# Gate and up products of four feed-forward layers as Strassen's seven block products, with the down product cut into five parts

## The chip, the cores and the metric

One core of one Trainium2 chip runs the whole program as a single launch. The metric is the device time of that launch in microseconds (us); smaller is better. The engines that matter here are PE (TensorE, the matrix engine, with PEld for its weight loads), DVE (VectorE), ACT (ScalarE), POOL (GpSimd) and SP (SyncE, which issues most DMAs).

## The reference, cut to what matters

A model of two blocks on 512 tokens of width 1024, all in fp32. The first block has two layers, each of them: a feed-forward, a mixer of three branches (Fourier, dilated attention, differential attention), and a second feed-forward. So there are four feed-forwards in the first block, and the change rewrites these. The second block (a mixer with delta rule and window attention, a cross attention to a memory, one more feed-forward) follows.

```python
D_MODEL = 1024; SEQ = 512; D_FF = 2816
def swiglu(h, w_gate, w_up, w_down):
    return (jax.nn.silu(h @ w_gate) * (h @ w_up)) @ w_down
# first block, per layer l
x = x + 0.5 * swiglu(rmsnorm(x, g_ffn1[l]), w_ffn1_gate[l], w_ffn1_up[l], w_ffn1_down[l])
...   # mixer
x = x + 0.5 * swiglu(rmsnorm(x, g_ffn2[l]), w_ffn2_gate[l], w_ffn2_up[l], w_ffn2_down[l])
```

## The kernel before

The activations lie transposed: `x[c]` is 128 channels by 512 tokens, c from 0 to 7. Every fp32 operand of a product is split into a high and a low fp32r part (`split`, line 299: ACT copies the high part, DVE subtracts it from the source for the low part), and each 128x128 block of weights takes three matmuls of 512 columns: high by high, high by low, low by high (`mm3`, line 351). Weights are fetched from HBM by SP into `raw` tiles of 128x1024 (pool of 3), and split into `whi` and `wlo` tiles of 128x512 (pools of 5 each). Most other tiles come from one pool of 128x512 tiles, `pg`, with NB = 63 of them (line 45).

A feed-forward (`ffn_task`, line 708) works in two halves of 11 column tiles of 128 out of the 22 of D_FF. For each column tile, `ffn_half` (line 675) forms the gate product and the up product, each 8 blocks of the inner dimension by 3 matmuls. Their operand is `us`, x times its gain, without the norm's factor; `evac` multiplies both results by the norm's row `rb` (`mul_rb`), takes silu on ACT, multiplies, and splits the product into `hs`. After a half comes its part of the down product: for each of 8 channel tiles, 11 blocks by 3 matmuls, added to x by DVE. In the second half `pre_chunk` (line 442) follows each channel tile: it makes the next stage's `us[c]` and adds its squares for the next norm, on POOL. The norm itself (`norm_task`, line 431) runs beside the first product of the next stage, `wide` (line 473), which makes four column tiles at a time.

The order of instructions is that of the program's own driver (`drive`, line 236): tasks are generators with a priority, they yield when their operands are due by a running estimate (`note`, line 192), and `acq`/`rel` (line 274) count the tiles of `pg` that a task may hold. The mixers start with a count of NB - 22 (line 829), the second block's mixer with NB - 30 less what the memory task holds (line 1447). Then a scheduler places the instructions on the engines, each of which runs its own in order. Two tasks, `setup_second` (line 1188: clears a scratch area in HBM by one DMA of 4.1 MB, loads masks, makes sine and cosine tables) and `memory` (line 2070: norm and transposes of the memory's 256 rows), are started with the last feed-forward of the first block and spread over it by waits of 20 to 60 us of planned time.

## Time and profile before

| | |
|---|---|
| time, median of 3 runs | 3449.64 us (3449.59 to 3451.47) |
| time of the profiled execution | 3459.29 us |
| its span | 3457.5 us |
| PE busy | 3356.0 us, 97% |
| PE weight loads busy | 2835.2 us, 82% |
| DVE busy | 1905.8 us, 55% |
| ACT busy | 1369.1 us, 40% |
| POOL busy | 337.6 us, 10% |

Busy times are of the profiled execution. Matmuls overlap each other in the pipeline, so the mean duration of one is longer than the distance from one start to the next; the distances are what a stage is made of. An instruction of DVE or ACT that waits for nothing also starts before the one ahead of it has ended. The four feed-forwards stand, by their weights' DMA issues, at about 0 to 368, 864 to 1230, 1230 to 1591 and 2088 to 2466 us.

### The profile page before, as it was taken

The page shows a single profiled execution, that of the slowest core. Times are in us where ns is not written, and L with a number is a line of the kernel's source. Part 1 is how long each engine was busy: PE and PEld are TensorE (multiplying, and loading weights), DVE is VectorE, ACT ScalarE, POOL GpSimd, SP SyncE. Part 2 cuts the span into 40 slices and gives each one's busy share as a digit, 9 for nine tenths or more (in the row PEclk, how much of TensorE's full clock was granted, in tenths as well). Part 3 has the DMA queues.
Part 4 walks back from the last instruction along what each step waited for, and adds up shares of the span by engine and source line. Part 5 has one row for each costly group of instructions (what it writes and reads, how often), then busy time and mean ns, then how long its engine had stood idle before and what let it go on. Part 6 is the DMA issues. An engine that isn't in the chain of part 4 may idle for free.

```text
span 3457.5 us, 44625 instructions
## 1 busy us (share of the span) xinstructions
PE 3356.0 (97%) x16759; PEld 2835.2 (82%) x16759; DVE 1905.8 (55%) x3644; ACT 1369.1 (40%) x2672; POOL 337.6 (10%) x325
## 2 busy tenths in 40 slices
PE   8999999999999999999999999999978889999998
PEld 7788888898888888888888987888867887788887
DVE  5444476656444444444767474545488764754344
ACT  4323445543332333234445443333354443443232
POOL 1000100000000000001000001000354433220001
PEclk9999999999999999999999999999999999999999
DMA  4533333435333333334333257333336453223232
GB/s 123 151 104 101 117 96 101 124 109 176 93 95 101 95 100 90 100 96 121 96 101 119 86 189 147 102 102 96 93 121 189 152 156 107 68 74 99 96 98 85
DMA packets 424422, 386.46 MB, mean 112 GB/s; under 512 B 31184, under 2 KB 379577, under 8 KB 424205
## 3 DMA queue, kind: packets, MB, share of 16 engines
q1 hardware_dynamic: 383584, 333.50, 32.2%
q10 hardware_dynamic: 40141, 48.54, 5.2%
q8 instruction: 131, 2.15, 0.3%
q0 software_dynamic: 480, 1.57, 0.1%
q14 instruction: 86, 0.70, 0.1%
HBM read 341.46 MB, written 37.88 MB: 110 GB/s over the span
## 4 chain that ended last, share of the span: by engine, by line
PE 90%; DVE 5%; DMA 2%; ACT 1%; issue 1%; POOL 0%; SPq 0%; ACTq 0%; DVEq 0%; POOLq 0%
PE ps L119 90%; DVE g L119 3%; DVE sm L119 1%; ACT g L119 1%; DVE wlo L119 0%; DMA raw<-in_w_ffn_gate 0%; ACT whi L119 0%; DVE tmp L119 0%; DMA g<-xinv_d 0%; DMA raw<-in_w_in 0%; DMA raw<-in_w_ffn_up 0%; DMA g<-cs_d 0%; ACT L119 0%; DMA g<-in_g_ffn 0%; DMA g<-in_x 0%
## 5 line engine op out<-in xcount | busy, mean ns | idle before, releaser
L119 PE MATMUL ps<-g,whi 128*128 128x512 f32 (+1 forms) x7776 | 2396.9, 390 | 19.7 <-ACT g L119 9.4
L119 PEld LDWEIGHTS ps<-g,whi 128*128 128x128 f32 x7776 | 1450.3, 189 | 314.1 <-ACT g L119 11.1
L119 PE MATMUL ps<-g,wlo 128*128 128x512 f32 (+1 forms) x3888 | 1508.6, 388 | 4.7 <-DVE wlo L119 2.8
L119 ACT ACTIVATE whi<-raw 128x512 fp32r<-128x512 f32 (+2 forms) x1100 | 673.0, 617 | 1347.2 <-PE ps L119 1216.8
L119 DVE TENSOR_TENSOR wlo<-raw,whi 128x512 fp32r<-128x512 f32 (+2 forms) x1038 | 706.3, 685 | 607.6 <-ACT whi L119 589.2
L119 PEld LDWEIGHTS ps<-g,wlo 128*128 128x128 f32 x3888 | 735.6, 189 | 157.2 <-DVE wlo L119 4.9
L119 DVE TENSOR_TENSOR g<-ps,g 128x512 f32<-128x512 f32 (+3 forms) x486 | 299.1, 625 | 422.9 <-PE ps L119 342.4
L119 DVE TENSOR_TENSOR g<-g,g 128x512 f32<-128x512 f32 (+3 forms) x494 | 352.9, 726 | 133.3 <-ACT g L119 124.7
L119 POOL TENSOR_TENSOR g<-g,g 128x512 f32<-128x512 f32 (+4 forms) x142 | 181.9, 1289 | 2142.7 <-ACT g L119 2088.8
L119 ACT ACTIVATE g<-g 128x512 fp32r<-128x512 f32 (+3 forms) x473 | 289.8, 617 | 206.3 <-DVE g L119 171.5
L119 PE MATMUL ps<-g,g 128*128 128x128 f32 (+6 forms) x1638 | 265.7, 310 | 19.0 <-ACT g L119 7.1
L119 PE MATMUL ps<-whi,g 128*128 128x256 f32 (+1 forms) x1184 | 259.2, 312 | 0.0
L119 PEld LDWEIGHTS ps<-g,g 128*128 128x128 f32 (+3 forms) x1638 | 224.2, 193 | 40.2 <-ACT g L119 8.5
L119 PEld LDWEIGHTS ps<-whi,g 128*128 128x128 f32 x1184 | 198.0, 193 | 11.4
L119 PE MATMUL ps<-wlo,g 128*128 128x256 f32 (+1 forms) x592 | 183.9, 311 | 0.0
L119 ACT ACTIVATE g<-ps 128x256 fp32r<-128x256 f32 (+6 forms) x231 | 95.6, 426 | 150.5 <-PE ps L119 128.2
L119 DVE SCALAR_TENSOR_TENSOR g<-ps,g 128x512 f32<-128x512 f32 x114 | 83.5, 734 | 103.7 <-PE ps L119 101.7
L119 PEld LDWEIGHTS ps<-wlo,g 128*128 128x128 f32 x592 | 114.3, 193 | 5.9
L119 POOL TENSOR_TENSOR wlo<-raw,whi 128x512 fp32r<-128x512 f32 x62 | 86.5, 1396 | 222.0 <-ACT whi L119 198.0
L119 ACT COPY g<-ps 128x512 f32<-128x512 f32 (+6 forms) x154 | 59.5, 417 | 111.2 <-PE ps L119 106.1
L119 ACT ACTIVATE g<-g,sm 128x512 f32<-128x512 f32 (+3 forms) x160 | 89.0, 579 | 31.2 <-DVE sm L119 28.3
L119 PE MATMUL ps<-ident,g 128*128 128x128 f32 (+1 forms) x491 | 79.1, 286 | 21.4 <-DVE g L119 12.2
(173 smaller groups left out, 1352.4 us busy)
## 6 DMA issues: line engine op xcount, KB each, us to landing
raw<-in_w_ffn_gate SPq DMA_DIRECT2D x87, 512.0 KB
raw<-in_w_ffn_up SPq DMA_DIRECT2D x87, 512.0 KB
raw<-in_w_in SPq DMA_DIRECT2D x80, 512.0 KB
raw<-in_w_ffn_down SPq DMA_DIRECT2D x64, 512.0 KB
raw<-in_w_gate SPq DMA_DIRECT2D x48, 512.0 KB
raw<-in_w_gate_up SPq DMA_DIRECT2D x44, 512.0 KB
raw<-in_w_ffn_down SPq DMA_DIRECT2D x64, 192.0 KB
gd<-g ACTq DMA_DIRECT2D x48, 256.0 KB
```

Of the source, the lines that this page charges most:

```text
L119: r = f(*a, **k)
```

## The change

In each of the four feed-forwards the column tiles 0 to 5 of D_FF are formed as before (tiles 0 and 1 by `wide`, tiles 2 and 3 from `us`; tiles 4 and 5 from the normed and split x that `fast_x` makes, so without the two multiplications by `rb`). The other 16 tiles are done in 8 groups of two, called quads here. For a quad the weights form a 2 by 2 block matrix (gate and up, by even and odd blocks of the inner dimension) and the tokens another (even and odd blocks, by first and second 256 tokens). Its eight block products become Strassen's seven, each of 2 x 4 x 3 = 24 matmuls of 256 columns. `fast_ops` makes the four sums of activations once per feed-forward. `fast_split` splits the weights of one product and forms four sums of weights per quad, each over 128x1024, on DVE. `fast_mm` lets several products add up in the same PSUM bank; ACT copies intermediate sums out of it, DVE adds and multiplies, `fast_end` splits the results into `hs`.

The down product is cut into five passes, over 6, 4, 4, 4 and 4 column tiles. The first four stand between the quads; only the last stands at the end. The sequence is a hand-written list of items, whose weights are split three items ahead of their matmuls. Between the second quad and the third there is no down product.

Around it: `raw` has 5 tiles for 3, `pg` 59 for 63, and a new tag `big` (4 tiles of 128x1024) serves the normed x and half of the quads' weights, and in the mixers what had tags of its own (`v`, `oa`, `vdh`, `vdl`). `setup_second` and `memory` wait until the last pass of the last of the four feed-forwards, and their waits become 5 to 10 us.

```diff
-NB = 63
+NB = 59
-        self.raw = mk("raw", bufs=3)
+        self.raw = mk("raw", bufs=5)
+    def big(self, dt=F32, shape=None):
+        return self.pp.tile(shape or [P, 2, S], dt, tag="big", bufs=4, name=self.nm("b"))
+    def fast_x(self, row):
+        xn = [[self.big() for _ in range(2)] for _ in range(2)]
+        xr = []
+        for c in range(KC):
+            t = xn[c % 2][c // 4][:, c // 2 % 2]
+            self.nc.vector.scalar_tensor_tensor(t, self.x[c], self.gcol(row, c), self.rb, ALU.mult, ALU.mult)
+            xr.append(self.split(t))
+        return xn, xr
+    def fast_ops(self, xn, xr):
...
+        for q in range(2):
+            b11, b12, b21, b22 = (xn[r][q][:, :, sl] for r in range(2) for sl in (one, two))
+            t = []
+            for i, a, b in ((5, b12, b11), (6, b22, None), (7, b22, b12), (4, b21, None)):
+                b = t[(i == 4)] if b is None else b
+                t.append(self.g(shape=[P, 2, 256]))
+                sub(a, b)
+                hi, lo = self.split(t[-1], self.g(F32R, [P, 2, 256]), self.g(F32R, [P, 2, 256]))
+                ops[i] += [(hi[:, k], lo[:, k]) for k in range(2)]
+    def fast_load(self, wg, wu, f):
...
+        for i, w, two in ((1, wg, 0), (2, wg, 1), (5, wu, 0), (4, wu, 1)):
+            q[i] = raw = self.big(shape=[P, 4, 256]) if two else self.raw.tile([P, 4, 256], F32, tag="raw", name=self.nm("raw"))
+            nc.sync.dma_start(raw, w[:, f * P:f * P + 256].rearrange("(p t k) c -> t k p c", t=2, k=P)[two])
+    def fast_split(self, q, i):
...
+        for g in range(2):
+            hi = self.whi.tile([P, 4, P], F32R, tag="whi", name=self.nm("whi"))
+            lo = self.wlo.tile([P, 4, P], F32R, tag="wlo", name=self.nm("wlo"))
+            w.append(self.split(q[i][:, :, g * P:(g + 1) * P], hi, lo))
+        tt = self.nc.vector.tensor_tensor
+        if i == 1:
+            q[7] = self.raw.tile([P, 4, 256], F32, tag="raw", name=self.nm("raw"))
+            tt(q[7], q[1], q[5], ALU.subtract)
+            tt(q[5], q[5], q[4], ALU.add)
+            q[6] = q[1]
+            tt(q[6], q[5], q[1], ALU.subtract)
+        elif i == 2:
+            q[3] = q[2]
+            tt(q[3], q[2], q[6], ALU.subtract)
+    def fast_mm(self, q, i, xs):
...
+        bank = {1: "a", 6: "a", 7: "a", 4: "a", 5: "b", 3: "b", 2: "c"}[i]
...
+                for n, (a, b) in enumerate(((hi, x[0]), (hi, x[1]), (lo, x[0]))):
+                    nc.tensor.matmul(o, a[:, k], b, start=first and (g, k, n) == (0, 0, 0),
+                                     stop=(g, k, n) == (1, 3, 2), skip_group_check=True)
+        if i in (1, 6, 7):
+            q["s", i] = t = self.g()
+            nc.scalar.copy(t, p)
+        elif i == 2:
+            t = q["s", 1]
+            nc.vector.tensor_tensor(t, t, p, ALU.add)
+            nc.scalar.activation(t, t, AF.Silu)
...
+    def fast_end(self, q, hs):
...
+        nc.vector.tensor_tensor(two, two, up, ALU.mult)
+        for g in range(2):
+            h = (self.g(F32R), self.g(F32R))
+            for k, t in enumerate((one, two)):
+                sl = slice(256 * k, 256 * k + 256)
+                self.split(t[:, 256 * g:256 * g + 256], h[0][:, sl], h[1][:, sl])
+            hs[q["n"] + g] = h
...
+        down(0, 6, (0,))
+        load(0)
+        down(0, 6, (2,))
+        for n in range(nq):
+            left(n, 1)
+            left(n, 2)
+            if n:
+                left(n - 1, 4)
+            left(n, 6)
+            left(n, 5)
+            if n + 1 < nq:
+                load(n + 1)
+            if n:
+                left(n - 1, 3)
+            left(n, 7)
+            if n == 0:
+                down(0, 6, (4, 6))
+            elif n > 1:
+                f = 6 + 4 * (n // 2 - 1)
+                if n + 1 < nq:
+                    down(f, f + 4, (4, 6) if n % 2 else (0, 2))
+                else:
+                    down(f, f + 4, (4,))
+                    left(n, 4)
+                    left(n, 3)
+                    down(f, f + 4, (6,))
+        items.append((lambda: setattr(self, "room", True), None))
+        down(FC - 4, FC, range(0, KC, 2))
+        ahead = 3
...
     def setup_second(self):
         nc, i = self.nc, self.i
+        yield lambda: self.room
...
-        yield 60.0
+        yield 5.0
...
-        yield 40.0
+        yield 5.0
...
     def memory(self):
         nc, i = self.nc, self.i
+        yield lambda: self.room
...
-            yield 60.0
+            yield 10.0 * t
...
-            yield 20.0
+            yield 5.0
```

`left(n, i)` is one product of quad n, numbered as in `fast_mm`; `down(f0, f1, cs)` is a pass over the column tiles f0 to f1 - 1, two channel tiles per item. Product 1 comes with three sums of weights (for products 7, 5 and 6), product 2 with one (for product 3).

## Rows read from the trace of the kernel before

**Rows 1.** The page's first part: engine, busy us, share, instructions.

```profile
PE 3356.0 (97%) x16759; PEld 2835.2 (82%) x16759; DVE 1905.8 (55%) x3644; ACT 1369.1 (40%) x2672; POOL 337.6 (10%) x325
```

**Rows 2.** The page's fourth part, the chain that ended last, by engine.

```profile
PE 90%; DVE 5%; DMA 2%; ACT 1%; issue 1%; POOL 0%; SPq 0%; ACTq 0%; DVEq 0%; POOLq 0%
```

**Rows 3.** Busy time by stretch: the four feed-forwards; columns in the first line.

```profile
core 0: us, PE busy (x) PEld busy (x) DVE busy (x) ACT busy (x) POOL busy (x), PEclk, DMA share, GB/s
0.00:368.00 368.00, 356.71 (x1561) 291.29 (x1562) 176.13 (x294) 130.10 (x216) 16.44 (x26) 1.00 0.42 120
865.00:1231.00 366.00, 366.00 (x1624) 303.28 (x1623) 166.15 (x262) 123.83 (x203) 11.68 (x9) 1.00 0.33 95
1231.00:1592.00 361.00, 361.00 (x1602) 299.16 (x1601) 162.86 (x257) 119.29 (x197) 9.08 (x7) 1.00 0.35 100
2088.00:2468.00 380.00, 372.89 (x1643) 305.16 (x1642) 184.54 (x321) 135.36 (x236) 18.61 (x14) 0.99 0.43 107
```

**Rows 4.** Timeline of PE in a feed-forward: start us, us, instruction, how many merged.

```profile
199.90 0.62 PE L119 MATMUL ps<-g,whi 128*128 128x512 f32 x2
...
202.62 0.62 PE L119 MATMUL ps<-g,whi 128*128 128x512 f32 x2
```

**Rows 5.** Timeline of PE in a mixer, matmuls of 256 columns.

```profile
423.77 0.40 PE L119 MATMUL ps<-whi,g 128*128 128x256 f32 x2
424.01 0.28 PE L119 MATMUL ps<-wlo,g 128*128 128x256 f32 x1
...
432.77 0.28 PE L119 MATMUL ps<-whi,g 128*128 128x256 f32 x1
```

**Rows 6.** The page's fifth part: weight loads of the matmuls of 256 columns.

```profile
L119 PEld LDWEIGHTS ps<-whi,g 128*128 128x128 f32 x1184 | 198.0, 193 | 11.4
```

**Rows 7.** DVE's groups by form: count, busy us, mean ns, idle before.

```profile
L119 DVE TENSOR_TENSOR wlo<-raw,whi 128x512 fp32r<-128x512 f32 x934 | 652.9, 703 | 543.5 <-ACT whi L119 525.0 <-PE ps L119 16.2 <-ACT g L119 0.7
L119 DVE TENSOR_TENSOR g<-ps,g 128x256 fp32r<-128x256 f32 x84 | 34.8, 421 | 28.9 <-ACT g L119 28.7
```

**Rows 8.** Timeline of DVE in a feed-forward.

```profile
217.78 0.69 DVE L119 TENSOR_TENSOR g<-ps,g 128x512 f32<-128x512 f32 x1 [1.59 <-PE ps L119]
218.38 0.68 DVE L119 TENSOR_TENSOR wlo<-raw,whi 128x512 fp32r<-128x512 f32 x1
218.98 0.69 DVE L119 TENSOR_TENSOR g<-g,g 128x512 f32<-128x512 f32 x1
```

**Rows 9.** ACT's groups by form.

```profile
L119 ACT ACTIVATE whi<-raw 128x512 fp32r<-128x512 f32 x996 | 624.2, 631 | 1245.1 <-PE ps L119 1137.3 <-DMA raw<-in_w_ffn_gate 19.7 <-issue 16.9
L119 ACT COPY g<-ps 128x512 f32<-128x512 f32 x63 | 36.6, 583 | 78.8 <-PE ps L119 78.8
```

**Rows 10.** Busy time by stretch in the second block's mixer and cross attention.

```profile
2620.00:2650.00 30.00, 27.19 (x165) 23.67 (x163) 28.33 (x83) 11.86 (x35) 8.71 (x9) 1.00 0.84 245
2468.00:3047.00 579.00, 515.47 (x3017) 445.69 (x3016) 398.81 (x850) 258.26 (x621) 221.60 (x179) 0.94 0.42 127
```

**Rows 11.** Timelines of ACT and DVE where the third feed-forward begins.

```profile
1258.59 0.59 ACT L119 COPY g<-ps 128x512 f32<-128x512 f32 x1 [8.03 <-PE ps L119]
1259.77 2.75 DVE L119 TENSOR_TENSOR wlo<-raw,whi 128x512 fp32r<-128x512 f32 x4 [3.22 <-ACT whi L119]
1270.18 0.69 DVE L119 TENSOR_TENSOR g<-ps,g 128x512 f32<-128x512 f32 x1 [7.66 <-PE ps L119]
```

**Rows 12.** Timelines and one stretch around the scratch area's clearing DMA.

```profile
2111.46 0.61 ACTq L119 DMA_DIRECT2D xinv_d<-g  x1
2144.36 1.22 PE L119 MATMUL ps<-g,whi 128*128 128x512 f32 x2 [6.42 <-ACT whi L119]
2137.00:2149.00 12.00, 5.58 (x17) 4.06 (x16) 4.08 (x7) 4.73 (x7) 0.00 (x0) 0.72 0.98 199
```

**Rows 13.** PE's waits in the second block's mixer and cross attention, longest sums first.

```profile
PE ps L119 <- ACT g L119: 19.0, 5, 6.1
PE ps L119 <- DVE g L119: 17.8, 7, 9.6
```

More of the change, by code (lines that the diff above doesn't have):

```diff
@@ L706, in ffn_half @@
             yield 0
-    def ffn_task(self, wg, wu, wd, row, after):
+    def fast_x(self, row):
[7 more added lines that the diff above has]
+    def fast_ops(self, xn, xr):
+        sub = lambda a, b: self.nc.vector.tensor_tensor(t[-1], a, b, ALU.subtract)
+        one, two = slice(0, 256), slice(256, S)
+        ops = [None] * 8
+        for i, r, sl in ((1, 0, one), (2, 1, one), (3, 1, two)):
+            ops[i] = [(xr[2 * k + r][0][:, sl], xr[2 * k + r][1][:, sl]) for k in range(KC // 2)]
+        for i in (4, 5, 6, 7):
+            ops[i] = []
+        for q in range(2):
[7 more added lines that the diff above has]
+                ops[i] += [(hi[:, k], lo[:, k]) for k in range(2)]
+        return ops
@@ L709, in ffn_task, with evac, left, right @@
+    def ffn_task(self, wg, wu, wd, pre, row, after):
         nc = self.nc
         us = self.us
-        n = FC // 2
-        for half in range(2):
-            hs = []
-            yield from self.ffn_half(us, wg, wu, half, hs)
-            for c in range(KC):
-                w = self.slab(wd[half * n * P:(half + 1) * n * P, c * P:(c + 1) * P], n, P)
-                pd = self.proj_t(w, 0, hs)
+        hs = {}
+        def evac(f, pg, pu, raw=True):
+            t, v = self.g(), self.g()
+            if raw:
+                self.mul_rb(t, pg)
+                self.mul_rb(v, pu)
+                nc.scalar.activation(t, t, AF.Silu)
+            else:
+                nc.scalar.activation(t, pg, AF.Silu)
+                v = pu
+            nc.vector.tensor_tensor(t, v, t, ALU.mult)
+            hs[f] = self.split(t)
+        ps = yield from self.wide((wg[:, 0:256], wu[:, 0:256]), us, 2 if self.t < 10.0 else 4)
+        late = [(f, ps[f], ps[2 + f]) for f in range(2)]
+        sg, su = self.slab(wg[:, 256:512], KC, 256), self.slab(wu[:, 256:512], KC, 256)
+        late.append((2, self.proj_t(sg, 0, us), self.proj_t(su, 0, us)))
+        yield 0
+        yield lambda: self.normed
+        xn, xr = self.fast_x(pre)
+        for x in late:
+            evac(*x)
+        evac(3, self.proj_t(sg, P, us), self.proj_t(su, P, us))
+        yield 0
+        sg, su = self.slab(wg[:, 512:768], KC, 256), self.slab(wu[:, 512:768], KC, 256)
+        evac(4, self.proj_t(sg, 0, xr), self.proj_t(su, 0, xr), False)
+        yield 0
+        xs = self.fast_ops(xn, xr)
+        evac(5, self.proj_t(sg, P, xr), self.proj_t(su, P, xr), False)
+        yield 0
+        nq = (FC - 6) // 2
+        quads, items = [], []
+        def left(n, i):
+            items.append((lambda: self.fast_split(quads[n], i), lambda: right(n, i)))
+        def right(n, i):
+            self.fast_mm(quads[n], i, xs)
+            if i == 7:
+                self.fast_sum(quads[n])
+            elif i == 3:
+                self.fast_end(quads[n], hs)
+                quads[n] = None
+        def down(f0, f1, cs):
+            for c in cs:
+                w = []
+                items.append((lambda c=c, w=w: w.extend(self.slab(wd[f0 * P:f1 * P, c * P:c * P + 256], f1 - f0, 256, True)),
+                              lambda c=c, w=w: product(f0, f1, c, w)))
+        def product(f0, f1, c0, w):
+            for c in (c0, c0 + 1):
+                pd = self.proj_t(w, (c - c0) * P, [hs[f] for f in range(f0, f1)])
@@ L721, in ffn_task @@
+        items.append((lambda: setattr(self, "room", True), None))
+        down(FC - 4, FC, range(0, KC, 2))
+        ahead = 3
+        for k in range(-ahead, len(items)):
+            if k + ahead < len(items):
+                items[k + ahead][0]()
+            if k >= 0 and items[k][1]:
+                items[k][1]()
                 yield 0
+        self.room = False
         after()
@@ L874, in mixer_task @@
         wv = w_in[:, c3 + 1024:c3 + 1536]
-        vs += [tuple(self.pp.tile([P, S], F32R, tag="v", bufs=2 * NT, name=self.nm("v")) for _ in range(2)) for _ in range(NT)]
+        for _ in range(0, NT, 2):
+            vh, vl = (self.big(F32R) for _ in range(2))
+            vs += [(vh[:, k], vl[:, k]) for k in range(2)]
         for o in range(0, 512, 256):
@@ L1805, in delta @@
         if oa[h] is None:
-            oa[h] = (self.pp.tile([P, S], F32, tag="oa", bufs=4, name=self.nm("oa")), set())
+            if h % 2 == 0 or oa[h ^ 1] is None:
+                pair = self.big()
+                oa[h & 2], oa[h | 1] = ((pair[:, k], set()) for k in range(2))
         oa, seen = oa[h]
@@ L1974, in window_v @@
         win["v"] = vd = []
+        his, los = (self.big(F32R, [P, NT, 2, 2, 64]) for _ in range(2))
         for k in range(NT):
-            hi, lo = self.pp.tile([P, 2, 2, 64], F32R, name=f"vdh{k}"), self.pp.tile([P, 2, 2, 64], F32R, name=f"vdl{k}")
+            hi, lo = his[:, k], los[:, k]
             src = p[:, k * P:(k + 1) * P].rearrange("p (v d) -> p v d", v=2).unsqueeze(2).to_broadcast([P, 2, 2, 64])
@@ L2397, in ffn @@
         w = [i[f"w_ffn{k}_{name}"][l] for name in ("gate", "up", "down")]
-        n.spawn(n.ffn_task(*w, row, after), 5)
+        n.spawn(n.ffn_task(*w, (G_FFN1, G_FFN2)[k - 1][l], row, after), 5)
     def ffn1(l):
```

37 lines of the change are left out of this document (36 added, 1 removed).

## The prediction

> **What bounds the kernel now.** I read the busy shares first: PE 97%, DVE 55%, ACT 40% [rows 1]. Then the chain that ended last: 90% of it is PE, 5% DVE [rows 2]; so time goes away only where PE's own stream gets shorter, or where a PE wait vanishes. The stretches of the four feed-forwards sharpen that: in the second and third PE is busy for all of the 366 and 361 us, DVE for 166 and 163 us, 45% [rows 3]. The first loses 11 us at the program's start, the fourth 7 us to one wait that is looked at below. What such a stretch costs is then a count of matmuls times the distance between their starts. Three matmuls of 512 columns start every 0.68 us (four groups of three from 199.90 to 202.62), 0.2267 us each [rows 4]. A feed-forward has 22 x 2 x 8 x 3 = 1056 for gate and up and 22 x 8 x 3 = 528 for down, 1584 in all: 359.1 us, which is the 361 us of the third.
>
> **The change, term by term.**
>
> *PE's stream.* 256-column matmuls start 75 in 9.00 us (423.77 to 432.77), 0.120 us each [rows 5]. Half of 0.2267 would be 0.1133, so each instruction carries some 0.013 us that doesn't shrink with its columns. A quad is 96 matmuls of 512 columns before, 96 x 0.2267 = 21.76 us, and 7 x 24 = 168 of 256 columns after, 20.16 us. Seven eighths would have been 19.04; the finer cut gives 1.1 us of the 2.7 back. What is left is 1.60 us per quad, 12.8 per feed-forward, **51.3 us** for 32 quads. The down product keeps its 528 matmuls.
>
> The Trainium skill speaks against the finer cut (TensorE: Matmul & The Clock Gate, "The mechanism"): a weight load overlaps matmuls in flight only when it goes to another row group, and here every load fills all rows. The trace disagrees: the loads last 0.193 us [rows 6] while the matmuls that they serve start 0.120 us apart [rows 5], so they do overlap. The rule's price is among the rivals.
>
> *DVE's load.* Does DVE hold that pace? A 128x512 operation lasts 0.69 us, but one that waits for nothing starts 0.60 after the last (217.78, 218.38, 218.98) [rows 8]. A 256-wide one lasts 0.42 [rows 7], so 256 more columns cost 0.27; the 1024-wide sums of weights have no row, and by these two are an estimated 0.60 + 2 x 0.27 = 1.14 apart, or 1.22 long. Per quad: 14 low parts of weights, 4 sums of weights, 5 sums or products on results, 4 half-width splits. With the short distances 14 x 0.60 + 4 x 1.14 + 5 x 0.60 + 4 x 0.33 = 17.3 us, with full durations 9.7 + 4.9 + 3.5 + 1.7 = 19.7 us; PE takes 20.16. Alone, a quad is therefore 86 to 98% DVE. The down items dilute it: one has 24 matmuls, 5.44 us of PE, for 2 low parts and 2 additions, 2.4 to 2.8 us of DVE, and there are two of them per quad from the third on (and larger ones after the first). A quad with its down items is 22 to 25 us of DVE in 31 of PE. ACT has 14 x 0.63 + 3 x 0.58 [rows 9] + 2 silu and 4 half-width copies, some 13 of 20 us: no bound.
>
> The Trainium skill says that a DVE operation doesn't start until the pipeline of the one before is empty (VectorE: DVE Perf Modes, "The DRAIN you can't avoid"). The starts 0.60 us apart under durations of 0.69 [rows 8] say that a part of it overlaps; by the rule the 19.7 would be the value to take, and the first rival below would be likelier.
>
> *Waits in the quads.* Each product's two weight tiles come from pools of five, so the second tile of the product three ahead gets a free buffer only in the middle of the next product. From there ACT's 0.63 and DVE's 0.69 pass, and about 3 us are left before PE wants it. Product 1 puts 1.2 to 1.4 + 3 x 1.14 to 1.22, about 5 us, into DVE's queue ahead of product 2's weights. With down products in front (two of 5.44 us) that is covered. At the third quad nothing stands in front: 14 products, 40.3 us of PE, hold 35 to 39 us of DVE, with the second quad's sums, the first quad's end (sum, silu on ACT, product, splits: 3 to 4 us in which DVE waits for ACT) and the weights of the following product queued together. Its DMA, too, comes late: the third load takes over a `big` tile that the first quad reads until its product 3 is split, which the list places after the load; three transfers of 0.52 MB queue behind that, 2.1 us each at the 245 GB/s that a stretch reaches [rows 10]. PE wants product 1 some 8.7 us and product 2 some 11.5 us later; DVE is through with the sums at 10 to 12. The stall lies between 0 (all of it fits) and 6 us (the end of the first quad delays two products); I take 2.5, nearer to the low end because the scheduler lets ready weight splits pass the waiting sums. Four times: **10 us**.
>
> *Start of a feed-forward.* The row `rb` is there at about 1259.2 (1258.59 + 0.59), halfway through `wide`, which ends at about 1270 [rows 11]. `fast_x` needs 16 DVE operations, 9.6 to 11 us from then on, and its result is wanted by tile 4, after tiles 2 and 3 with 10.9 us each, at 1292. The sums of activations (16 more) have tiles 4 and 5 and two down items of 8.2 us as cover. So nothing, or at most 1 us where the first weight split of tile 2 stands behind `fast_x`: 0.5 each, **2 us**.
>
> *End of a feed-forward.* The last pass has 12 matmuls, 2.72 us, per channel tile for 33 before. DVE needs 3 operations there (addition, `us`, a low part), 1.8 to 2.1 us: covered, no cost. In the fourth feed-forward `pre_chunk` adds a fourth, so 2.4 to 2.8 us, and exactly there `setup_second` (12 full-width operations, 7 us) and `memory` are now let in. Some 5 us of DVE work spill into the next stage. The clearing DMA moves there as well. Before, issued at 2111.46, it held up weights until PE had stood for 6.4 us, and the clock granted after it was down to a mean of 0.72 in 12 us [rows 12]. I expect the same stall at its new place, a little less with 5 `raw` tiles and a little more with a busy DVE: no change, bounds -10 and +10.
>
> *The smaller pool.* With 59 tiles the mixers plan with 37 for 41, the second mixer with 18 or 19 for 23, one of the tasks that hold five or six less at a time. The first block's mixers hardly idle and have gate products to fill with: 0 to 5 each, taken 1.5, **3 us**. The second block's stretch idles for 579 - 515 = 64 us, behind single dependencies of up to 6.1 us on ACT and 9.6 on DVE [rows 10, 13], and one of these may come again: -5 to +25, I take **5 us**, about one such wait.
>
> *Sum.* -51.3 + 10 + 2 + 3 + 5 = -31 us. The profiled execution would come from 3459.3 to 3428 us, and the median, 9.7 below it, from 3449.6 to **3418.5 us**.
>
> **Rivals.**
>
> *DVE becomes the bound (slower).* Places: products 1 and 2 of every quad, where DVE has 7 of the quad's 17 to 20 us in a row, and product 3, where it waits for silu. If that chain makes PE stand in each quad and not only in the third, it decides from 1.6 us per quad on, the whole gain. At 3 us, a first quad's end without cover, it costs 96: 3449.6 - 51.3 + 96 + 10 = 3504 us. For it: 86 to 98% in a bare quad. Against: 71 to 81% with the down items, and PE's three items of weights in hand. 13%.
>
> *The rest of the program gives it back.* The smaller pool takes one task at a time out of the second mixer, or the clearing DMA meets that mixer's first weights, or the last pass overfills DVE. With +20 on the mixer and +10 on the end instead of 5, the sum is -51.3 + 15 + 30 = -6: 3443 us, 3436 to 3457. For it: the 64 us idle there show a chain that isn't covered. Against: the memory's products are its filler and remain. 15%.
>
> *No stall at all.* The scheduler fills DVE's queue so that the third quad costs nothing, and the fourth feed-forward's old stall of 6.4 us and its slow clock vanish with the five `raw` tiles: -51.3 - 10 = 3388 us. 12%.
>
> *The finer matmuls don't overlap their loads.* The skill's rule from above. Here a quad has 72 loads more than before; at 0.193 us [rows 6] all uncovered, 13.9 us per quad, 445 in all: 3449.6 - 51.3 + 445 = 3843 us with the old ones left hidden. The 0.120 us of rows 5 stand against it. 1%.
>
> **How the numbers follow.** The forecast has 59%, with a range of its own of 3398 to 3436. About 0.2% of the time, 6.9 us, is what a measurement of this kernel can tell from no change: 3442.7 to 3456.5. Faster: forecast 59, no stall 12, half of the give-back 7: 78%. Same: the rest of the give-back and the mildest case of DVE: 9%. Slower: 13%. The range from 3390 to 3455 holds the forecast, most of the give-back and half of the no-stall case.
>
> **What would show it.** In the profile after: 5376 more PE matmuls of 256 columns and 3072 fewer of 512; starts 0.120 us apart inside a product. In a stretch of a quad with its two down items PE without idle time and DVE at 70 to 80%; between the first quads PE waits on `wlo` or `ps` of a few us per feed-forward. DVE's busy time up by some 80 to 110 us per feed-forward. Wrong would be the forecast if PE's idle rows name DVE in every quad (the first rival), if the distance inside the new products is above 0.13 (1344 x 4 x 0.01 = 54 us, the gain), or if the feed-forwards are shorter by 11 us each and the second block longer by more than 20.

## The result, and the profile after

The changed kernel takes 3471.9 us (median of 4 runs, 3469.76 to 3477.94), the kernel before 3450.18 us (4 runs, 3449.59 to 3451.47): a ratio of 1.0065, 95% interval 1.0048 to 1.0083. It is slower by 0.65%, where 3418.5 us was forecast, and outside the range of 3390 to 3455. Its profiled execution took 3472.75 us, with a span of 3471.0.

The page's first and fourth parts of the kernel after (engine, busy us, share, instructions; then the chain that ended last), which answer to [rows 1] and [rows 2]:

```profile
PE 3329.1 (96%) x19063; PEld 2918.2 (84%) x19063; DVE 2298.2 (66%) x4188; ACT 1576.6 (45%) x3072; POOL 337.1 (10%) x325
...
PE 84%; DVE 7%; DMA 2%; ACT 2%; issue 1%; POOL 0%; SPq 0%; ACTq 0%; DVEq 0%; POOLq 0%
```

PE issues 2304 matmuls more, which is 5376 of 256 columns less 3072 of 512, as the change says, and it is busy for 26.9 us less. The span is 13.5 us longer all the same, so PE idles some 40 us more. PE's share of the chain falls by 6 points, and DVE and ACT gain three between them. (The profiled execution of before was 9.1 us above its median, that of after 0.9; only these executions have traces, so the comparison of stages below is made in spans, 3457.5 against 3471.0.)

Where did it go? Each stage begins with a norm, and a norm's sum shows on PE as the first small matmuls against a tile of ones. Four of these on PE's timeline of the kernel before (start us, us, engine, instruction, how many merged):

```profile
391.66 0.94 PE L119 MATMUL ps<-ones,g 128*128 128x1 f32 x8
...
892.90 0.95 PE L119 MATMUL ps<-ones,g 128*128 128x1 f32 x8
...
1253.82 0.95 PE L119 MATMUL ps<-ones,g 128*128 128x1 f32 x8
...
3065.03 0.95 PE L119 MATMUL ps<-ones,g 128*128 128x1 f32 x8
```

The same four in the kernel after:

```profile
399.02 0.95 PE L119 MATMUL ps<-ones,g 128*128 128x1 f32 x8
...
898.23 0.95 PE L119 MATMUL ps<-ones,g 128*128 128x1 f32 x8
...
1247.59 0.95 PE L119 MATMUL ps<-ones,g 128*128 128x1 f32 x8
...
3075.76 0.95 PE L119 MATMUL ps<-ones,g 128*128 128x1 f32 x8
```

The second feed-forward lies between the second and the third: 360.9 us before, 349.4 after. Worked out in the same way for every stage, in us:

| stage | before | after | difference |
|---|---|---|---|
| first feed-forward | 391.7 | 399.0 | +7.3 |
| first mixer | 501.2 | 499.2 | -2.0 |
| second feed-forward | 360.9 | 349.4 | -11.5 |
| third feed-forward | 360.9 | 349.3 | -11.6 |
| second mixer of the first block | 501.2 | 498.6 | -2.6 |
| fourth feed-forward | 374.4 | 393.2 | +18.8 |
| second block: mixer and cross attention | 574.7 | 587.1 | +12.4 |
| the rest | 392.5 | 395.2 | +2.7 |

So the change does what it says where nothing else is going on, and it is given back in two places: beside the first feed-forward, where 18.8 us are missing against the 11.5 due, and from the fourth feed-forward on, where fourth and second block together are 31.2 longer instead of 11.5 shorter, 42.7 us. The border between these two moves with the place of one norm, so they are taken together from here on: 949.1 us before, 980.2 after.

Busy time by stretch of the kernel after (columns in the first line): first to fourth feed-forward, then the second block's start and the rest of it, beside [rows 3] and [rows 10]:

```profile
core 0: us, PE busy (x) PEld busy (x) DVE busy (x) ACT busy (x) POOL busy (x), PEclk, DMA share, GB/s
0.00:364.00 364.00, 338.16 (x2078) 300.34 (x2079) 257.17 (x407) 169.59 (x297) 11.40 (x22) 0.98 0.40 118
862.00:1212.00 350.00, 349.67 (x2169) 315.79 (x2168) 252.18 (x381) 167.46 (x289) 9.36 (x7) 1.00 0.34 100
1212.00:1562.00 350.00, 349.67 (x2184) 316.36 (x2183) 260.25 (x395) 171.03 (x298) 9.92 (x7) 1.00 0.33 100
...
2412.00:2470.00 58.00, 42.18 (x174) 33.53 (x173) 38.85 (x72) 22.95 (x47) 14.45 (x11) 0.85 0.70 117
2470.00:3048.00 578.00, 496.88 (x2867) 430.24 (x2866) 397.34 (x858) 255.15 (x617) 213.72 (x175) 0.91 0.39 122
```

In the second and third feed-forward PE is busy for 349.67 of 350 us, with DVE at 72 to 74%: no stall in any quad. The first has 26 us of idle PE for 11 before. The second block idles 81 of 578 us for 64 of 579 before, and the granted clock, a mean of 0.91 for 0.94, falls with it.

The timeline of PE inside a quad of the kernel after, beside [rows 5]:

```profile
1439.82 0.40 PE L119 MATMUL ps<-g,whi 128*128 128x256 f32 x2
1440.06 0.28 PE L119 MATMUL ps<-g,wlo 128*128 128x256 f32 x1
...
1444.86 0.40 PE L119 MATMUL ps<-g,whi 128*128 128x256 f32 x2
```

42 matmuls in 5.04 us: 0.120 each, the price that the prediction took from the mixer.

### The profile page after: what moved, and what is told of

Same layout as the page of the kernel before. It is cut to its first block, busy times and chain, and to the rows that moved or that the text cites. A ratio compares the mean times of both kernels' runs of the same rounds, so it can differ in the third digit from the quotient of the medians.

```text
span 3471.0 us, 50601 instructions
## 1 busy us (share of the span) xinstructions
PE 3329.1 (96%) x19063; PEld 2918.2 (84%) x19063; DVE 2298.2 (66%) x4188; ACT 1576.6 (45%) x3072; POOL 337.1 (10%) x325
## 4 chain that ended last, share of the span: by engine, by line
PE 84%; DVE 7%; DMA 2%; ACT 2%; issue 1%; POOL 0%; SPq 0%; ACTq 0%; DVEq 0%; POOLq 0%
PE ps L119 84%; DVE g L119 5%; ACT g L119 1%; DVE sm L119 1%; DVE wlo L119 1%; DMA g<-in_positions 0%; POOL g L119 0%; DMA g<-g 0%; SPq L119 0%; DMA b<-in_w_ffn_up 0%; DMA g<-xinv_d 0%; DMA raw<-in_w_ckv 0%; DMA g<-kn_d 0%; DMA g<-cs_d 0%; DVE b L119 0%
## 5 line engine op out<-in xcount | busy, mean ns | idle before, releaser
L119 PEld LDWEIGHTS ps<-g,whi 128*128 128x128 f32 x9312 | 1629.6, 191 | 241.3 <-ACT g L119 19.0
L119 PE MATMUL ps<-g,wlo 128*128 128x512 f32 (+1 forms) x4656 | 1622.2, 348 | 17.5 <-DVE wlo L119 16.5
L119 ACT ACTIVATE whi<-raw 128x512 fp32r<-128x512 f32 (+1 forms) x1084 | 669.9, 622 | 867.4 <-PE ps L119 766.5
L119 PEld LDWEIGHTS ps<-g,wlo 128*128 128x128 f32 x4656 | 890.1, 191 | 130.5 <-DVE wlo L119 18.6
L119 DVE TENSOR_TENSOR wlo<-raw,whi 128x512 fp32r<-128x512 f32 (+1 forms) x1022 | 707.4, 700 | 395.4 <-ACT whi L119 382.2
L119 ACT ACTIVATE g<-g 128x256 fp32r<-128x256 f32 (+4 forms) x561 | 311.6, 571 | 221.9 <-DVE g L119 171.4
L119 DVE TENSOR_TENSOR g<-g,g 128x512 f32<-128x512 f32 (+4 forms) x550 | 346.7, 650 | 90.2 <-ACT g L119 80.1
L119 ACT ACTIVATE whi<-b 128x512 fp32r<-128x512 f32 x192 | 121.2, 632 | 225.5 <-PE ps L119 213.4
L119 ACT COPY g<-ps 128x512 f32<-128x512 f32 (+5 forms) x250 | 114.3, 476 | 138.2 <-PE ps L119 125.9
L119 DVE TENSOR_TENSOR wlo<-b,whi 128x512 fp32r<-128x512 f32 x192 | 131.8, 688 | 53.8 <-ACT whi L119 53.3
```

Source lines behind the costliest of these rows:

```text
L119: r = f(*a, **k)
```

## The experiments

Two theories, with a common part. The common part is that the quads give about 11.5 us each time. *The count*: the pool is smaller by four tiles, the second block's mixer plans with a count smaller by four, and its order of work comes out worse. *The late guests*: `setup_second` and `memory`, which now wait for the end of the fourth feed-forward, hold up the second block's first norm. Beside them stood a third for the first feed-forward: `setup_task`, which the change doesn't touch, meets a pool that is now full.

The kernel before was run again beside each group of experiments: 3452.90 us beside the pool alone and the three on late guests, 3450.69 beside the two with the old count alone, the earlier first load and the three repairs, 3455.76 beside the other four. Each ratio is to the runs beside it, so kernels of different groups are better compared by ratio than by time; the stages come from one profiled execution of each kernel.

### The pool alone

The kernel before with 59 tiles for 63.

```diff
-NB = 63
+NB = 59
```

> The kernel before with one number changed, 59 tiles in pg for 63, and nothing of Strassen. In the changed kernel the time from the first block's last norm sums to the end of the program is about 15 us longer than before (982.3 for 967.1 us), and the four feed-forwards saved 11.5 us each only where no other task ran in them. Theory of the late guests (setup_second and memory are let in at the last pass, and DVE then stands behind a DMA): the pool alone does little, 3450 to 3454 us. Theory of the small pool (the mixers plan with four tiles less and leave PE idle): 3460 to 3475 us, with the second block's stretch longer by 10 us or more.

Measured: 3481.47 us, ratio 1.0085 (1.007 to 1.01), above both ranges. Fourth feed-forward and second block take 977.9 us for 949.1: 29 us from four tiles, before any part of Strassen is in. The first block's mixers become shorter, 498.7 and 498.9 for 501.2 each, so the prediction's +1.5 for each of them has the wrong sign. The loss is in the second block alone.

### Are the late guests the cause?

The kernel after, with the positions' first DVE operation 60 us of planned time later.

```diff
         nc.scalar.dma_start(pi, i["positions_2"][0].partition_broadcast(P))
+        yield 60.0
         ang = self.g()
         nc.vector.tensor_copy(ang, pi)
```

> The changed kernel with one wait more: setup_second issues the positions' DMA where it did, and the first DVE operation on them comes 60 us of planned time later. Late guests: DVE no longer stands 12.4 us (2431.9 to 2444.3) in front of the last pass's additions, PE's wait of 13.4 us at 2433 goes, and the norm of the second block comes 15 to 25 us earlier: 3447 to 3460 us. Small pool: 3470 to 3474 us, since what follows doesn't depend on that wait.

What it is aimed at, in the timelines of the kernel after (in square brackets the idle time before an instruction and what ended it), ordered by time over ACT's queue, DVE and PE:

```profile
2401.23 0.61 ACTq L119 DMA_DIRECT2D xinv_d<-g  x1
...
2428.08 6.63 ACTq L119 DMA_DIRECT2D g<-in_positions  x1
...
2431.20 0.68 DVE L119 SCALAR_TENSOR_TENSOR g<-ps,g 128x512 f32<-128x512 f32 x1
...
2444.32 0.43 DVE L119 CAST g<-g 128x512 f32<-128x512 int32 x1 [12.44 <-DMA g<-in_positions]
...
2446.98 0.47 PE L119 MATMUL ps<-ident,g 128*128 128x128 f32 x1 [13.39 <-DVE g L119]
...
2488.69 1.84 PE L119 MATMUL ps<-ones,g 128*128 128x1 f32 x16
```

The clearing DMA, which writes 4.1 MB, is issued at 2401.23. The positions, 0.26 MB, are issued 27 us later on the same queue and come only behind it. DVE, which runs its instructions in order, stands at the CAST for 12.44 us with the residual's work behind it, and PE waits 13.39. The norm's sum follows at 2488.69. With the edit it comes at 2462.80:

```profile
2462.80 3.16 PE L119 MATMUL ps<-ones,g 128*128 128x1 f32 x16
...
3075.39 0.95 PE L119 MATMUL ps<-ones,g 128*128 128x1 f32 x8
```

That is 26 us earlier, and the end of the second block doesn't move: 3075.39 for 3075.76. Measured: 3474.21 us, 1.0064 (1.0049 to 1.0079), the kernel after again. So this wait, the most striking one of the trace, is not what sets the end.

The next two move the guests' work instead of one wait: first the clearing DMA to the start of the fourth feed-forward with the rest left late, then all of `setup_second` back to where it was before.

```diff
     def setup_second(self):
-        yield lambda: self.room
         self.xinv = ...
         nc.scalar.dma_start(self.xinv..., z...)
+        del z                          # first kernel only
+        yield lambda: self.room        # first kernel only
-        yield 5.0                      # second kernel only, from here
+        yield 60.0
...
-        yield 5.0
+        yield 40.0
         pi = self.g(I32)
```

> The changed kernel with the scratch area's clearing DMA back at the start of the fourth feed-forward, as before; masks, positions and memory still wait for the last pass. The positions then have a free queue and land in 2 to 4 us. Late guests: most of the 12.4 us of DVE goes, but the old wait for weights behind the clearing DMA (6.4 us and a slow clock) may come back in the feed-forward: 3450 to 3465 us. Small pool: 3470 to 3474 us.

> The changed kernel with the whole of setup_second started at the beginning of the fourth feed-forward with its old waits of 60 and 40 us; memory alone still waits for the last pass. Late guests: no late DMA ahead of DVE and 7 us less of DVE work in the last pass: 3440 to 3455 us. Small pool: 3468 to 3474 us; it could even be slower, if the four tiles that setup_second holds are missing in the quads.

Measured: 3460.72 us, 1.0025 (1.0015 to 1.0034), and 3457.75 us, 1.0012 (1.0003 to 1.0022). Fourth feed-forward and second block: 965.6 and 966.0 for 980.2. The clearing DMA's place is worth some 15 us and that of the rest nothing that shows; two thirds of the 42.7 us remain. In the first of the two all of this lies in the fourth feed-forward, 378.5 us for 393.2, while the second block keeps its 587.1 us and runs its work in the same order about 12 us sooner; so there it is not a better order. In the second the order of the second block changes as well. Its time, 3457.75 us, lies between the ranges of both theories.

### Real tiles or the planner's count?

Before with 59 tiles, but the second block's mixer planning as if there were 63; the kernel after with the same line; and the reverse, before with its 63 tiles and a count of 59.

```diff
# first and second kernel
-        self.free = NB - 16 - 9 - 5 - self.mem
+        self.free = NB + 4 - 16 - 9 - 5 - self.mem
# third kernel, on before, NB = 63
+        self.free = NB - 4 - 16 - 9 - 5 - self.mem
```

> The kernel before with 59 tiles in pg, as in the run with the pool alone (3481.5 us), but the second block's mixer plans as with 63: its count starts at NB + 4 - 30 less what memory holds. Theory of the count: with four tiles less in the count the mixer's head projections can't be acquired in time, memory's products (priority 7) run instead, at 2562 to 2605 us for 2635 to 2812, and are missing as filler later; the real tiles matter little: 3450 to 3460 us, and memory's products spread again. Theory of the real tiles (instructions wait for a free one of 59): 3474 to 3485 us, as without the edit.

> The changed kernel with the same single edit: the second block's mixer plans with four tiles more than the pool gives. Count: the second block's stretch, 587 us from the norm sums at its head to those at its end, loses most of the 29 us that the pool alone cost: 3443 to 3456 us. Real tiles: 3468 to 3475 us. A third outcome, 3457 to 3467 us, would say that the late setup of the second block binds the same stretch a second time.

> The kernel before with its 63 tiles in pg, and only the second block's mixer counting four fewer: the reverse of the run with 59 tiles and the old count (3448.2 us). Theory of the count: 3474 to 3485 us, as with the small pool itself (3481.5), and memory's products early again. Theory of the real tiles: 3448 to 3455 us.

Measured, with fourth feed-forward and second block in us behind the ratio:

| kernel | tiles | count | median us | ratio | stage |
|---|---|---|---|---|---|
| before | 63 | 63 | 3450.18 | 1 | 949.1 |
| before, fewer tiles | 59 | 59 | 3481.47 | 1.0085 (1.007 to 1.01) | 977.9 |
| before, fewer tiles, old count | 59 | 63 | 3448.15 | 0.9988 (0.9979 to 0.9998) | 944.0 |
| before, lower count alone | 63 | 59 | 3487.81 | 1.0094 (1.0079 to 1.0109) | 980.1 |
| after | 59 | 59 | 3471.90 | 1.0065 (1.0048 to 1.0083) | 980.2 |
| after, old count | 59 | 63 | 3436.44 | 0.9954 (0.9939 to 0.9969) | 940.3 |

All four corners of the table for the kernel before say the same: the four tiles cost nothing (the stage is 2 to 5 us shorter with 59), the four in the count cost 31.0 us of the stage with 63 tiles and 33.9 with 59. In the kernel after one line gives 35.5 us back in the medians, 39.9 in this stage of the profiled executions, and it then beats the kernel before, with 3436.44 us below every range that was named for it. (The two runs on the kernel before lie 2 us below and 3 us above the ranges of the theory of the count.) This is the main cause.

How a count does that is seen in three rows of each trace, with the first and the last start in us. The first is the stores of the memory's products on POOL's queue (keys and values for the cross attention, `kv_d`), six of them. The second is the loads of the solved blocks (`xinv_d`), with which each of the eight delta-rule chains of the mixer begins. The third is the 32 score operations of the window attention on DVE (they read its mask, `m_win`). The fences are, in this order: the kernel before, the one with the lower count alone, the kernel after, and after with the old count.

```profile
L119 POOL DMA_DIRECT2D kv_d<-g x6: 582/584/767, 2635.1 to 2811.6; - x6
L119 SPq DMA_DIRECT2D g<-xinv_d x16: 359/582/2650, 2639.7 to 2822.6; - x16
L119 DVE CUSTOM_DVE_ANT_0 g<-ps,m_win x32: 411/486/558, 2720.0 to 2815.2; 128x256 f32<-128x256 f32 x16, 128x384 f32<-128x384 f32 x16
```

```profile
L119 POOL DMA_DIRECT2D kv_d<-g x6: 559/582/770, 2568.4 to 2612.5; - x6
L119 SPq DMA_DIRECT2D g<-xinv_d x16: 359/502/1461, 2655.1 to 2737.4; - x16
L119 DVE CUSTOM_DVE_ANT_0 g<-ps,m_win x32: 419/488/559, 2840.3 to 2896.4; 128x256 f32<-128x256 f32 x16, 128x384 f32<-128x384 f32 x16
```

```profile
L119 POOL DMA_DIRECT2D kv_d<-g x6: 557/580/767, 2624.1 to 2757.8; - x6
L119 SPq DMA_DIRECT2D g<-xinv_d x16: 360/458/920, 2629.5 to 2724.0; - x16
L119 DVE CUSTOM_DVE_ANT_0 g<-ps,m_win x32: 414/488/558, 2821.7 to 2876.9; 128x256 f32<-128x256 f32 x16, 128x384 f32<-128x384 f32 x16
```

```profile
L119 POOL DMA_DIRECT2D kv_d<-g x6: 559/587/767, 2624.1 to 2786.7; - x6
L119 SPq DMA_DIRECT2D g<-xinv_d x16: 370/458/1626, 2629.3 to 2795.8; - x16
L119 DVE CUSTOM_DVE_ANT_0 g<-ps,m_win x32: 418/488/559, 2702.3 to 2822.5; 128x256 f32<-128x256 f32 x16, 128x384 f32<-128x384 f32 x16
```

The memory's products need nothing from the mixer, so they can fill any gap of PE, and with the smaller count they run earlier. But the larger change is in the mixer's own order. With a count of 63 the window attention lies among the delta chains, whose last steps (the last tile `vw` that DVE copies) come behind it, at 2879 and 2852 us. With 59 all eight chains are through first, with their last `vw` at 2797 and 2780, and the window attention comes behind them, packed into some 55 us with little beside it. The code offers a reason, which no run tested by itself: `window_proj` asks for 12 tiles of the count at once, a delta chain for 6, so with fewer in the count the chains are served first.

What the count costs is lost between 2800 and 2890. Busy time of that stretch in the kernel before, with the lower count alone, after, and after with the old count:

```profile
2800.00:2890.00 90.00, 79.69 (x575) 72.50 (x575) 52.81 (x138) 30.20 (x77) 25.18 (x23) 0.94 0.47 144
```

```profile
2800.00:2890.00 90.00, 65.62 (x299) 57.58 (x298) 63.76 (x186) 47.51 (x118) 17.13 (x12) 0.77 0.16 49
```

```profile
2800.00:2890.00 90.00, 61.03 (x282) 54.04 (x281) 64.80 (x217) 53.54 (x144) 7.75 (x6) 0.73 0.09 27
```

```profile
2800.00:2890.00 90.00, 84.50 (x518) 73.19 (x518) 44.84 (x119) 34.64 (x80) 18.28 (x15) 0.98 0.33 107
```

With the count of 63, 360 and 260 of the 575 and 518 matmuls there are those of the last delta chains; of the memory's products 48 matmuls stand there in the kernel before and none in the other, whose last store is at 2786.7. So the memory's products are at most a small part of what the stretch has lost. With 59 the stretch holds no matmul of a delta chain and little DMA (a share of 0.09 and 0.16, for 0.33 and 0.47), and PE waits for the window attention. Here are PE's transposes of the softmax's results in the same stretch, in the kernel before and after (count, busy us, mean ns, idle time before them):

```profile
L119 PE MATMUL ps<-ident,g 128*128 128x128 f32 x28 | 3.5, 272 | 0.0
...
L119 PE MATMUL ps<-ident,g 128*128 128x128 f32 x80 | 17.6, 407 | 21.4 <-ACT g L119 21.4
```

PE's busy time of 61 to 66 us in the poor cases even flatters them, since the granted clock is down to 0.73 to 0.77, and a transpose takes 407 ns for 272. The other traces agree. In six of the seven kernels with a count of 59 the last score operation starts between 2864 and 2897, in all six with a count of 63 between 2800 and 2823; the seventh, with the early `setup_second`, lies between at 2860. The norm's sum at the end of the second block follows the last score operation by 199 to 200 us in each of the six with 59, and by 214 to 250 us with 63, where the chains end later. No run moved the window attention alone, so this order is seen beside the loss and not tested as its cause; the count is.

### More than 63?

```diff
-        self.free = NB - 16 - 9 - 5 - self.mem
+        self.free = NB + 8 - 16 - 9 - 5 - self.mem
```

> The changed kernel with the second mixer's count four higher still (as with 67 tiles). If more in flight is simply better there: below the 3436.4 us of the count of 63, 3425 to 3434 us. If the order is good only near the count that it was tuned with: above 3440 us. If the real 59 tiles now limit: 3436 to 3445 us, with waits for tiles in place of waits for the count.

Measured: 3454.43 us, 1.0001 (0.9991 to 1.001); stage 958.0. So 67 is 18 us worse than 63 (0.5% by the ratios), and better than 59. Here five of the memory's six products are stored only from 2771 to 2813, as late as in the kernel before, and PE is busy for 72.76 us from 2800 to 2890. The eight delta chains have begun by 2732 and the window attention's scores run from 2778 to 2858, so again most of it stands behind them, though the memory's products are late. The count is no "more is better": it turns the planner's order. Why 67 gives this order was not followed further.

### The first feed-forward

The kernel after waits here for something that the change doesn't touch. Its longest wait, a row of PE's waits from 60 to 130 us (us in total, times, longest), with the ACT rows and the PE row that belong to it:

```profile
PE ps L119 <- DMA g<-in_g_ffn_post: 6.7, 1, 6.7
```

```profile
80.25 0.53 ACTq L119 DMA_DIRECT2D g<-in_g_final  x1
...
82.89 0.31 ACTq L119 DMA_DIRECT2D g<-in_g_ffn_post  x1
...
84.48 0.45 PE L119 MATMUL ps<-ident,g 128*128 128x128 f32 x1 [6.67 <-DMA g<-in_g_ffn_post]
```

`setup_task` takes tiles of the pool, loads rows of gains into them, and has PE transpose them 10 us of planned time later. The first load and the transpose in the kernel before:

```profile
69.44 0.53 ACTq L119 DMA_DIRECT2D g<-in_g_final  x1
...
76.78 0.27 PE L119 MATMUL ps<-ident,g 128*128 128x128 f32 x1
```

The loads come 10.8 us later now, and the transpose, placed in PE's order by the plan, holds up everything behind it. Two things can make them late. `fast_x` and `fast_ops` take tiles of the pool in the same stretch, and POOL clears the task's tile at 60.50 us for 40.33 before. But ACT issues the loads only 20 us after that (29 before): they stand behind other work of ACT, which now has the eight splits of `fast_x` as well. Which of the two it is was not tested. Two edits: the first load 28 us of planned time earlier; and besides that, on the kernel with the old count, all of the task's distances between load and use widened.

```diff
     def setup_task(self):
-        yield 40.0
+        yield 12.0
...
-        yield 10.0        # second kernel only, at each of its five places
+        yield 30.0
```

> The changed kernel with setup_task of the first feed-forward started at 12 us of planned time for 40, so its gains' tile is taken before the normed x and its parts fill the pool. If that tile's lateness cost the first feed-forward its saving (PE's in-order queue waits 6.7 us at 77.8 for the DMA of those rows, and the end's norm sums come at 399 us for 392 before, where the two undisturbed feed-forwards saved 11.5 us): the wait goes, the norm sums come at 383 to 392, and the time falls by 7 to 16 us to 3456 to 3465. If other waits of the same task take its place (103 to 111 us): 3466 to 3474.

> The changed kernel with the second mixer's count as with 63 (alone 3436.4 us), and setup_task of the first feed-forward spread out: start at 12 us of planned time for 40, 30 us for 10 between a DMA's issue and the PE or DVE operation that needs it. If the first feed-forward lost its saving because PE's in-order queue stands behind that task's late tiles (waits of 6.7, 1.7, 2.3 us; the single earlier start only moved the wait to the next of its DMAs, 4.1 us), the excess of PE between 60 and 130 us falls from 20 us to below 6, the norm sums at its end come at 381 to 388 us, and the time is 3418 to 3427. If it is the full pool itself, other waits appear there: 3430 to 3440 us.

Measured: 3465.04 us, 1.004 (1.0026 to 1.0054), at the edge of the first range, and 3425.84 us, 0.9914 (0.9897 to 0.993), the latter against 3436.44 (0.9954) with the old count alone. The first feed-forward ends at 395.0 and 390.0 for 399.0 in the kernel after and 401.0 with the old count alone. (Among the kernels that leave this task as it is, it ends at 398.4 to 402.2.) Busy time from 60 to 130 us in the kernel before, after, and with the wider distances:

```profile
60.00:130.00 70.00, 70.00 (x303) 55.28 (x302) 39.78 (x70) 27.86 (x44) 0.20 (x1) 1.00 0.41 114
```

```profile
60.00:130.00 70.00, 57.41 (x244) 44.12 (x244) 50.70 (x85) 28.80 (x47) 0.21 (x1) 0.88 0.32 91
```

```profile
60.00:130.00 70.00, 65.86 (x337) 55.90 (x336) 57.79 (x97) 36.34 (x59) 0.00 (x0) 0.98 0.37 104
```

The idle time falls from 12.6 to 4.1 us, and the clock comes back from 0.88 to 0.98. With the earlier load alone the wait for the gains goes, and the next one of the same task takes its place:

```profile
84.76 1.87 PE L119 MATMUL ps<-g,g 32*10 32x512 f32 x2 [4.08 <-DMA g<-in_oneh]
```

That places about half of the loss at this task: of the 18.8 us, 9 come back, or 11 against the kernel with the old count alone. Of the others, two pieces are seen with the wide distances: 4.1 us of idle PE from 60 to 130 us and 4.3 from 260 to 300, where before it has none. So the 380 us of an undisturbed feed-forward (391.7 less 11.5) were not reached, nor the 381 to 388 expected, and what the rest is stays open.

### All together

The count with the early `setup_second` and the early first load; then the count with the early `setup_second` and the wide distances.

> The changed kernel with three repairs: setup_second at the beginning of the fourth feed-forward with its old waits (alone 3457.8 us), the second mixer's count as with 63 tiles, setup_task at 12 us. If the quads themselves save 11.5 us per feed-forward and the rest was these three: 3457.8 - 25 - 10, 3415 to 3432 us, faster than the kernel before. If the causes overlap in the second block's chain: 3435 to 3450 us.

> The run before the last of this list with setup_second at the beginning of the fourth feed-forward as well, with its old waits. If letting it in late still costs something once the count is right (the fourth feed-forward's norm sums come 367 us after the third's with the early start, 389 with the late one): 3405 to 3418 us. If PE has other work to do while that norm is late, as the two runs at 3433.6 and 3436.4 us suggest: 3415 to 3426 us, no more than 4 us from the run with the late start.

Measured: 3433.56 us, 0.9945 (0.993 to 0.996), and 3423.44 us, 0.9908 (0.9893 to 0.9923). The gains don't add; the first lies between its two ranges, and its first feed-forward ends at 398.2, so the early first load alone gives little there. `setup_second` early gave 14 us to the kernel after; on top of the old count and the wide distances it gives 2.4 (3425.84 to 3423.44, whose intervals overlap), though the second block's first norm comes some 24 us sooner with it (fourth feed-forward 366.3 for 389.6; the second block is longer by 20.7). The reading that fits these is that late guests cost PE little as long as it has other work while it waits. In the kernel after, the early `setup_second` also changed the order that the count sets (the window attention's scores start at 2711 for 2822); the early clearing DMA alone did not, and gave as much. 3423.44 us is the fastest of the study, 0.9% under the kernel before.

## Why the prediction was wrong, step by step

**What bounds the kernel, and the quads: right, the terms roughly to size.** The distance of 0.120 us came out to the digit, and with it the load times of 193 ns stayed hidden. The undisturbed feed-forwards save 11.5 us; the terms were 12.8 for the matmuls less 2.5 for the third quad and 0.5 for the start, 9.8 net. The stall of the third quad, "between 0 ... and 6 us", of which 2.5 were taken, is at the low end: 0.33 us of idle PE in 350. The reason that it gives for the low end, that ready weight splits pass the waiting sums, was not tested. DVE's busy time rose by 86 and 97 us in the second and third feed-forward, forecast at 80 to 110. It is 78% busy from 1380 to 1420 us, between quads and down items, where 71 to 81% was worked out. The 1024-wide sums, which had no row before, have one now:

```profile
L119 DVE TENSOR_TENSOR raw<-raw,raw 128x1024 f32<-128x1024 f32 x64 | 78.3, 1224 | 1.9
```

1224 ns each, as in "1.22 long".

**The smaller pool: this step failed.** Its term of 5 us for the second block stands against 29 us when the pool alone was changed and the 40 that the old count gave back in the changed kernel; even its upper bound of 25 was too low. The error is in how it was bounded: "one of the tasks that hold five or six less at a time" was priced as one more wait of the kind that the old trace shows [rows 13]. But a count doesn't add a wait to an order that stays; it makes another order. The task that has to wait here is the window attention, which then runs behind all eight delta chains and alone, and PE stands 21.4 us before its transposes. What the term needed was the question of which work would come last if one task has to wait, and what would then run beside it. The rival's "Against: the memory's products are its filler and remain" does not hold either: with the lower count alone all six are stored by 2612.5 us, where the last came at 2811.6 before. But keeping them late is no remedy: with a count of 67 they come late and the stage still takes 958.0 us. For the first block's mixers the sign was wrong as well, -2.0 and -2.6 us for +1.5 each; pool alone gave -2.5 and -2.3.

**A step that isn't there: `setup_task`.** The prediction went past the first feed-forward with "Start of a feed-forward", 0.5 us, as if all four were alike. The first has a task beside it with tiles from the same pool and with matmuls in PE's order, and it lost 18.8 us against the others, of which 9 to 11 were traced to that task. The old trace has nothing of it, since there PE is busy for all of the 70 us from 60 to 130; the change's demand for tiles and for ACT's queue could have been counted at this place.

**The late guests: named, and priced too low as a wait.** "I expect the same stall at its new place": 6.4 us were taken from [rows 12], and 13.4 came, since another load of the same queue now stood behind the clearing DMA and DVE stood at that load. That chain was not seen ahead. At the end of the program the term of 0 is right only in part: 0 us came where the wait alone was taken away and 2.4 us once the count was right, but the clearing DMA's place was worth 15 us in the kernel after, all in the fourth feed-forward. Why these don't agree stays open.

**The rivals.** "The rest of the program gives it back" was the right place, with the smaller pool at its head, and it had 15%; its price, up to 20 us on the mixer, was half of what came, and so it ended at 3443 and not at 3472. The sign "shorter by 11 us each and the second block longer by more than 20", named as what would make the forecast wrong, is in part what the profile shows: two of the four are shorter by 11.5, and the fourth with the second block is 31.2 longer. DVE as the bound and matmuls that don't overlap their loads are out by the 349.67 of 350 us. The sum, in spans: -31 was forecast, +13.5 came, 44.5 apart (44.9 by the parts, which are rounded). The smaller pool's term makes 35 of these (40 for 5), the first feed-forward 18.8, the rest of the fourth's and the second block's loss 2.7 (42.7 less 40), the last stage 2.7; against them stand 6.7 for the quads (4 x 11.5 for 39.3) and 7.6 for the first block's mixers (-4.6 for +3). The other 8 us of the difference in the medians, +21.7, lie in how the two profiled executions stand to their medians.

With the count put back and the task's distances widened, the kernel takes 3425.84 us, 3423.44 with the early setup: inside the forecast's own range of 3398 to 3436. The quads' gain was there in the two undisturbed feed-forwards all the time.

## What to carry to other kernels

When a change takes memory from a pool whose size also feeds a planner, price the two apart: whether the tiles themselves are short, and what order the planner makes of the smaller number. Ask which task would be pushed to the end, and whether anything would then be left to run beside it. And of several like stages look at each for what runs beside it: an unrelated task that shares the pool and ACT's queue, and puts matmuls into PE's in-order stream, can take back most of what the stage saves.

## What the runs showed of the hardware

Matmuls of 256 columns keep their distance of 0.120 us inside a quad, over 42 in a row. The clearing DMA of 4.1 MB, in rows of 516 bytes, lasted from 2402.6 to 2443.2 us in the kernel after, about 100 GB/s. The load of 0.26 MB issued on the same queue at 2428.08 was there only at 2444.3: 16 us, with 6.63 us for its issue by ACT alone. The granted clock was lower where PE stood idle more: a mean of 0.73 in the 90 us from 2800 in which PE was busy for 61.03 us, and 0.98 where the order of work gave it 84.50. Transposes of 128x128 lasted 407 ns in the first case and 272 ns in the second.
